# Eleven loads of weight sums on another DMA queue, and two products swapped, in an fp32-accurate streaming-encoder block on one Trainium2 core

## The chip, the cores and the metric

One core of a Trainium2 chip. The metric is the device time of one execution in microseconds; lower is better. The kernel is one program of 16129 instructions on TensorE (PE, with its weight loads listed as PEld), VectorE (DVE), ScalarE (ACT), GpSimd (POOL) and SyncE (SP). SP, ACT and POOL also issue DMAs, each through a queue of its own (SPq, ACTq; POOL's issues are listed as POOL).

## The reference

One layer over 512 tokens of width 1024, all in float32:

```
x = x + 0.5 * swiglu(rms_norm(x, ffn1_norm), gate1, up1, down1)
x = x + hybrid_mixer(rms_norm(x, mix_norm), ...)
x = x + 0.5 * swiglu(rms_norm(x, ffn2_norm), gate2, up2, down2)
return rms_norm(x, final_norm)
swiglu(h) = (silu(h @ w_gate) * (h @ w_up)) @ w_down
```

The hidden width of each feed-forward part (FFN) is 2816, that is 22 tiles of 128 or 11 pairs of tiles. The mixer (a projection, a state-space scan of 16 heads, chunked attention of 8 heads and an output projection) lies between the two FFNs, from about 300 to 700 us; the change doesn't touch it.

## The kernel before

**Split operands.** Each matrix product is made of three matmuls (`mm3`, L141 to L144, and L554 to L556): weight high part by activation high and low part, weight low part by activation high part. Each weight tile in SBUF is therefore split before use: ACT writes the high part (L272), DVE the rest (L274). `usplit` (L267) does so for the FFNs; its results rotate through four slots, so a split waits until PE is done with the tile four splits before.

**Seven products in place of eight.** In an FFN most of the work is a two-by-two block product done with seven products, P1 to P7 (Winograd's form of Strassen's scheme). Some need sums of weight blocks. They are made by DMAs that add into SBUF. For P5 of a pair of tiles d a buffer `view(d)` gets a first load (`first`, L329, a plain DMA) and one addition (`more`, L332, a DMA of POOL with `accum_op=add`). Once P5's split has read it, another addition makes P6's sum (L356), and once P6's split has read it, another makes P3's (L361). P7's sum is made the same way in a tile that P1 loaded (L358). P1, P2 and P4 use plain tiles (tag `raw`, four buffers, loaded through SP, L326). There are four such views; a new one takes the place of the one four before it, so its first load waits until the split of that one's P3 is done (`before`, L347 and L353).

**Order of the products.** `program` (L281) writes the order out by hand. With `plain` = 2 (FFN1) two pairs are done as plain products (A11 to A22) and pair 2 is the first by seven products; with `plain` = 1 (FFN2) pair 0 is plain. Then, pair by pair, come P5 and P1 of the next pair, P3 and P4 of this one, P6, P2, P7 of the next. After pairs 4 and 8 the products of a down block follow (the seven products again, on the down projection, steps "S", each with one or two half blocks written as (block, first pair)). FFN2 ends with a third down block whose second half has a view of its own for P6 (`LAST`, L349 to L354): a first load and two additions, with no split between them. In all 11 first loads are for down blocks, named `s<-ws` in the trace, and 19 for pairs (`s<-wgu`).

**Banks.** `run` (L545) gives a pair three PSUM banks: X for P1, P6, P7 and P4, L for P2, H for P5 and P3. ACT copies P1's (L560) and P6's (L563) result out of X, and the next product in X can't start before that. In the trace X is `mm`, L and H are `aux`.

**When things are issued.** `Stream.get` (L127) hands out the tiles in the order of the list, splits three ahead (`ws.look`), and issues a load or addition at most so many products ahead as its lead says (12 for a pair's first load, 14 for the last view's, 5 to 10 for others). The text of the program is, however, only a priority. A planner puts each instruction on its engine's queue when, by its own costs, its inputs and buffers are ready and the engine is free, the earlier in the text first. On the chip each queue then runs in that fixed order.

Of the kernel before, what the change touches and what calls it, by code (L numbers as in the profile page):

```python
# [37 lines left out]
def hybrid_block(ctx: ExitStack, tc, xT, xt, par, wgu1, wd1, ws1, win, wdt, wv, wo, rbt, wgu2, ws2, fin, out):  # L38
    nc = tc.nc
    V, S, G, T = nc.vector, nc.scalar, nc.gpsimd, nc.tensor  # L40
# [4 lines left out]
    def sb(tag, shape, dt=F32, bufs=1):  # L45
        uid[0] += 1
        return pool.tile(shape, dt, tag=tag, name=f"{tag}_{uid[0]}", bufs=bufs)
# [62 lines left out]
    class Stream:  # L110
# [16 lines left out]
        def get(self):  # L127
            i = self.used
            self.used += 1
            while self.done < min(len(self.jobs), i + 1 + self.look):  # L130
                job = self.jobs[self.done]
                job.move(0, True)
                job.parts = job.split()
                self.done += 1
            for n in range(self.done, min(len(self.jobs), i + 18)):
                self.jobs[n].move(n - i)
            return self.jobs[i].parts
# [95 lines left out]
    def wide_tile(g, dt=F32R):  # L233
        if g not in wide or wide[g][0] != dt:
            wide[g] = dt, sb(f"s{g}", [P, GROUPS[g], SEQ], dt)
        return wide[g][1]
# [30 lines left out]
    def usplit(src):  # L267

        i = turn[0] % 4
        turn[0] += 1  # L270
        hi = sb(f"xw{2 * i}", list(src.shape), F32R)
        S.copy(out=hi, in_=src)  # L272
        lo = sb(f"xw{2 * i + 1}", list(src.shape), F32R)
        V.tensor_tensor(out=lo, in0=src, in1=f(hi), op=ALU.subtract)  # L274
        return hi, lo
# [5 lines left out]
    def program(plain, by_tokens):  # L281


        if plain == 1:
            out = [("A11", 0), ("A21", 0), ("A12", 0), ("P1", 1), ("P5", 1), ("A22", 0), ("P6", 1), ("P2", 1), ("P7", 1)]
        else:
            out = [(a, d) for d in range(plain) for a in ("A11", "A21", "A12", "A22")]
            out += [(p, plain) for p in ("P5", "P1", "P6", "P2", "P7")]
        out = [("P", p, d) for p, d in out]
        ends = [b for _, b in BLOCKS[:2]]  # L290
        for d in range(plain + 1, ND):
            if d - 1 not in ends:
                out += [("P", p, e) for p, e in (("P5", d), ("P1", d), ("P3", d - 1), ("P4", d - 1))]
            out += [("P", p, d) for p in ("P6", "P2", "P7")]
            if d in ends:

                down = [("S", ends.index(d), p, (0, 1)) for p in DOWN]
                out += down[:1] + [("P", p, d) for p in ("P3", "P4")] + down[1:6]
                out += [("P", p, d + 1) for p in ("P5", "P1")] + down[6:]
        last = [("P", p, ND - 1) for p in ("P3", "P4")]  # L300
        if by_tokens == 3:
            return out + [("S", 2, "P5", (0,))] + last + [("S", 2, p, (0,)) for p in ("P1", "P2")] + [
                ("S", 2, p, (1,)) for p in ("P1", "P5")] + [("S", 2, "P6", (0, 1)), ("S", 2, "P2", (1,))] + [
                ("S", 2, p, (0, 1)) for p in ("P7", "P3", "P4")]
        out += [("D", 2, 0, 0)] + last + [("D", 2, 1, 0), ("D", 2, 0, 1), ("D", 2, 1, 1)]
        return out + [("D", 2, o, c) for o in range(2, KD) for c in range(2)]

    def ffn_weights(wgu, plain, by_tokens, wst, wd=None):


        bufs, jobs, views = {}, {}, []
        LAST = (2, ND - 1)

        def view(d):
            if d not in bufs:
                i = views.index(d)
                m = 2 if type(d) is int else min(2, BLOCKS[d[0]][1] - d[1])
                bufs[d] = wide_tile((40, 52)[i // 2 % 2], F32)[:, 2 * (i % 2):2 * (i % 2) + m]
                if type(d) is int:
                    bufs[d] = bufs[d].rearrange("p a (k c) -> p a k c", c=P)  # L320
            return bufs[d]

        def whole(key, src):
            def go():
                bufs[key] = sb("raw", list(src.shape), bufs=4)
                nc.sync.dma_start(out=bufs[key], in_=src)  # L326
            return go

        def first(d, src):  # L329
            return lambda: nc.sync.dma_start(out=view(d), in_=src)  # L330

        def more(get, src):  # L332
            return lambda: G.dma_start(out=get(), in_=src, accum_op=ALU.add)  # L333

        def product(p, d, A):

            sum_ = lambda: view(d)
            raw = {"P1": "g", "P2": "g2", "P4": "u2"}.get(p)
            if p[0] == "A":
                n = ("A11", "A12", "A21", "A22").index(p)  # L340
                j = Job(lambda: usplit(bufs[p, d]), (6, "raw", whole((p, d), A[n])))
            elif raw:
                j = Job(lambda: usplit(bufs[raw, d]), (6 if p == "P1" else 5, "raw",
                                                       whole((raw, d), A[("P1", "P2", "", "P4").index(p)])))
            elif p == "P5":
                views.append(d)
                before = jobs["P3", views[-5]] if len(views) > 4 else jobs.get(("A21", 0))  # L347
                j = Job(lambda: usplit(view(d)), (12, before, first(d, A[2])), (7, None, more(sum_, A[3])))
            elif p == "P6" and d == LAST:  # L349

                v = d + (2,)
                views.append(v)
                j = Job(lambda: usplit(view(v)), (14, jobs["P3", views[-5]], first(v, A[2])),  # L353
                        (10, None, more(lambda: view(v), A[3])), (6, None, more(lambda: view(v), A[0])))  # L354
            elif p == "P6":
                j = Job(lambda: usplit(view(d)), (6, jobs["P5", d], more(sum_, A[0])))  # L356
            elif p == "P7":
                j = Job(lambda: usplit(bufs["g", d]), (6, jobs["P1", d], more(lambda: bufs["g", d], A[2])))  # L358
            else:
                v = d + (2,) if d == LAST else d  # L360
                j = Job(lambda: usplit(view(v)), (6, jobs["P6", d], more(lambda: view(v), A[1])))  # L361
            jobs[p, d] = j
            if p == "P7":
                jobs["P1", d].holds = j
            ws.jobs.append(j)

        for step in program(plain, by_tokens):
            if step[0] == "P":
                p, d = step[1:]
                product(p, d, wgu[d])  # L370
            elif step[0] == "S":
                n, p, pieces = step[1:]
                for a in [BLOCKS[n][0] + 2 * c for c in pieces]:
                    product(p, (n, a), [wst[i, :, a:min(a + 2, BLOCKS[n][1]), :] for i in range(4)])
            else:
                n, o, c = step[1:]
                if c == 0:
                    a, b = 2 * BLOCKS[n][0], 2 * BLOCKS[n][1]
                    ws.add(wd[o, :, a:b, :], b - a, P)
                    late = ws.jobs.pop() if (n, o) in ((2, 0), (2, 1)) else None  # L380
                    if late:
                        jobs["late", o] = late
                elif ("late", o) in jobs and n == 2:
                    ws.jobs.append(jobs["late", o])
# [70 lines left out]
    def ffn(xc, n_plain, early, by_tokens, rc, between, after):  # L455
# [177 lines left out]
        pss = {}  # L633
        past = False
        for step in program(n_plain, by_tokens):
            if step[0] == "S":
                n, p, pieces = step[1:]
# [793 lines left out]
```

## Time and profile before

| | |
|---|---|
| median of 3 runs | 1032.14 us (1031.85 to 1036.27) |
| profiled execution | 1035.34 us |
| its span, first to last instruction | 1033.6 us |
| mean granted TensorE clock | 0.993 of full |
| PE busy | 1007.9 us, 98% of the span |
| DVE, ACT, POOL busy | 810.2, 587.8, 163.7 us |
| DMA through SP's and ACT's queues / POOL's | 96.74 + 4.86 MB / 60.04 MB |

The times are of executions of the whole program. The profiled execution is one more, 3.2 us above the median of the others; all durations of single instructions come from it. Times in the rows are microseconds from the start of its span, durations of groups nanoseconds. PE is busy nearly throughout, so the rows of interest are those in which it waits or runs at a lower clock.

### The profile page before, as it was taken

The numbers are of one execution on the slowest core, as the hardware profiler recorded it, in microseconds if no ns is written. First come the engines' busy times: TensorE is split into PE (matmuls) and PEld (weight loads), VectorE is DVE, ScalarE is ACT, GpSimd is POOL, SyncE is SP. The second block draws the span as 40 slices with busy tenths as digits, with TensorE's granted clock in tenths as the row PEclk, the third lists the DMA queues.
The fourth block names the chain that finished last, engine by engine and source line by source line (L and its number), as shares of the span: only waits on it lengthen the run. The fifth ranks groups of instructions, "written<-read, shape, count | busy, mean of one in ns | idle before, by whom it ended". The sixth has DMA issues, their size and how long they took to land. (4 is left out here: it accounts for less than half of the span.)

```text
span 1033.6 us, 16129 instructions
## 1 busy us (share of the span) xinstructions
PE 1007.9 (98%) x6154; PEld 888.6 (86%) x6154; DVE 810.2 (78%) x1353; ACT 587.8 (57%) x926; POOL 163.7 (16%) x186
## 2 busy tenths in 40 slices
PE   8999999999999999999999999999999999999895
PEld 7889989998898777778878778879999899988884
DVE  7868876887676698978867999797688668876587
ACT  7555535654474456646656876666655356544445
POOL 1111121111110013323201111101211111111110
PEclk9999999999999999999999999999999999999988
DMA  8969989998652321222232223755898889988842
GB/s 309 290 160 210 218 185 228 224 203 211 147 122 91 102 82 62 71 73 69 71 98 71 82 83 102 230 131 128 191 211 209 196 209 231 209 213 202 167 107 99
DMA packets 48221, 162.66 MB, mean 157 GB/s; under 512 B 5264, under 2 KB 6032, under 8 KB 48144
## 3 DMA queue, kind: packets, MB, share of 16 engines
q0 software_dynamic: 16848, 60.04, 33.2%
q1 hardware_dynamic: 28992, 96.74, 27.1%
q10 hardware_dynamic: 2304, 4.86, 1.5%
q8 instruction: 48, 0.79, 0.3%
q14 instruction: 29, 0.24, 0.1%
HBM read 159.52 MB, written 2.10 MB: 156 GB/s over the span
## 5 line engine op out<-in xcount | busy, mean ns | idle before, releaser
L555 PE MATMUL mm<-s,xw 128*128 128x256 f32 x1824 | 231.6, 284 | 6.4 <-ACT fu L563 4.6
L555 PEld LDWEIGHTS mm<-s,xw 128*128 128x128 f32 x1824 | 224.9, 192 | 7.6 <-ACT fu L563 5.0
L272 ACT CAST xw<-raw 128x1024 fp32r<-128x1024 f32 (+1 forms) x127 | 131.5, 1036 | 138.3 <-PE mm L555 56.0
L274 DVE TENSOR_TENSOR xw<-raw,xw 128x1024 fp32r<-128x1024 f32 (+1 forms) x127 | 152.7, 1204 | 69.4 <-ACT xw L272 69.4
L555 PE MATMUL aux<-s,xw 128*128 128x256 f32 x1368 | 174.5, 283 | 0.6 <-DVE xw L274 0.6
L555 PEld LDWEIGHTS aux<-s,xw 128*128 128x128 f32 x1368 | 169.0, 192 | 1.9 <-DVE xw L274 0.8
L142 PE MATMUL mm<-xw,whi 128*128 128x512 f32 x364 | 149.1, 410 | 0.0
L143 PE MATMUL mm<-xw,whi 128*128 128x512 f32 x364 | 144.3, 397 | 0.0
L274 DVE TENSOR_TENSOR xw<-s,xw 128x1024 fp32r<-128x1024 f32 (+1 forms) x87 | 104.6, 1202 | 50.5 <-ACT xw L272 50.4
L144 PE MATMUL mm<-xw,wlo 128*128 128x512 f32 x364 | 144.0, 396 | 0.0
L272 ACT CAST xw<-s 128x1024 fp32r<-128x1024 f32 (+1 forms) x87 | 90.0, 1035 | 92.1 <-DMA s<-wgu 27.7
L333 POOL DMA_DIRECT2D s<-wgu x57 | 52.1, 934 | 314.6 <-DMA s<-wgu 133.6
L84 ACT CAST whi<-raw 128x512 fp32r<-128x512 f32 (+1 forms) x104 | 62.1, 601 | 65.3 <-PE mm L143 47.2
L86 DVE TENSOR_TENSOR wlo<-raw,whi 128x512 fp32r<-128x512 f32 (+1 forms) x104 | 74.3, 716 | 13.8 <-ACT whi L84 13.2
L142 PEld LDWEIGHTS mm<-xw,whi 128*128 128x128 f32 x364 | 68.5, 188 | 16.2 <-issue 2.2
L144 PEld LDWEIGHTS mm<-xw,wlo 128*128 128x128 f32 x364 | 68.4, 188 | 16.1
L143 PEld LDWEIGHTS mm<-xw,whi 128*128 128x128 f32 x364 | 68.5, 188 | 15.8 <-issue 1.2
L333 POOL DMA_DIRECT2D s<-ws x31 | 27.1, 873 | 163.3 <-DVE xw L274 65.8
L144 PE MATMUL aux<-xw,s 128*128 128x512 f32 x106 | 41.8, 394 | 0.0
L143 PE MATMUL aux<-xw,s 128*128 128x512 f32 x106 | 41.7, 394 | 0.0
L142 PE MATMUL aux<-xw,s 128*128 128x512 f32 x106 | 41.7, 394 | 0.0
L903 POOL TENSOR_TENSOR fu<-dt,tri 128x512 fp32r<-128x512 f32 x16 | 18.9, 1190 | 95.6 <-PE aux L954 45.5
(294 smaller groups left out, 1743.9 us busy)
## 6 DMA issues: line engine op xcount, KB each, us to landing
raw<-wgu SPq DMA_DIRECT2D x68, 512.0 KB, 5.8
s<-wgu POOLq DMA_DIRECT2D x57, 512.0 KB, 6.5
raw<-win SPq DMA_DIRECT2D x28, 512.0 KB, 3.5
s<-ws POOLq DMA_DIRECT2D x27, 512.0 KB, 5.7
raw<-ws SPq DMA_DIRECT2D x27, 512.0 KB, 4.7
s<-wgu SPq DMA_DIRECT2D x19, 512.0 KB, 5.0
raw<-wgu POOLq DMA_DIRECT2D x19, 512.0 KB, 6.2
raw<-wo SPq DMA_DIRECT2D x12, 512.0 KB, 3.7
```

Of the source, the lines that this page charges most:

```text
L84: S.copy(out=hi, in_=src)
L86: V.tensor_tensor(out=lo, in0=src, in1=f(hi), op=ALU.subtract)
L142: T.matmul(ps, lhsT=sh, rhs=mh, start=start, stop=False, skip_group_check=skip)
L143: T.matmul(ps, lhsT=sh, rhs=ml, start=False, stop=False, skip_group_check=skip)
L144: T.matmul(ps, lhsT=sl, rhs=mh, start=False, stop=stop, skip_group_check=skip)
L272: S.copy(out=hi, in_=src)
L274: V.tensor_tensor(out=lo, in0=src, in1=f(hi), op=ALU.subtract)
L333: return lambda: G.dma_start(out=get(), in_=src, accum_op=ALU.add)
L555: T.matmul(ps[:, j * HS:(j + 1) * HS], lhsT=sw[:, j, k], rhs=m, start=(p in ("P1", "P2", "P5") and j == 0 and k == 0 and n == 0), stop=(k ...
L903: G.tensor_tensor(out=r, in0=f(src[:, c, h0:h0 + 4]).unsqueeze(2).broadcast_to([P, 4, P]), in1=tri.unsqueeze(1).broadcast_to([P, 4, P]), o ...
```

## The change

The first loads of down blocks go through POOL's queue in place of SP's: for a pair `d` is a number, for a down block a pair of numbers, and the test tells these apart. In FFN1's first pair by seven products (pair 2; the branch for `plain` = 1 is another) P2 comes before P6. Since the list of loads and splits and the order of the matmuls both come from `program`, both follow.

```diff
@@ in program
         else:
             out = [(a, d) for d in range(plain) for a in ("A11", "A21", "A12", "A22")]
-            out += [(p, plain) for p in ("P5", "P1", "P6", "P2", "P7")]
+            out += [(p, plain) for p in ("P5", "P1", "P2", "P6", "P7")]
         out = [("P", p, d) for p, d in out]
@@ in ffn_weights
         def first(d, src):
-            return lambda: nc.sync.dma_start(out=view(d), in_=src)
+
+            q = nc.sync if type(d) is int else G
+            return lambda: q.dma_start(out=view(d), in_=src)
```

## Rows read from the trace of the kernel before

**Rows 1.** The page, busy us of each engine (share of the span) and instructions
```profile
PE 1007.9 (98%) x6154; PEld 888.6 (86%) x6154; DVE 810.2 (78%) x1353; ACT 587.8 (57%) x926; POOL 163.7 (16%) x186
```

**Rows 2.** Stretches: busy us of PE, PEld, DVE, ACT, POOL; PEclk, DMA share, GB/s
```profile
60.00:80.00 20.00, 18.21 (x148) 17.82 (x149) 13.83 (x19) 11.24 (x15) 3.52 (x4) 1.00 0.73 175
...
980.00:985.00 5.00, 2.39 (x11) 2.39 (x12) 2.89 (x5) 3.00 (x4) 0.00 (x0) 0.56 0.30 58
985.00:990.00 5.00, 5.00 (x25) 4.57 (x25) 3.31 (x4) 2.06 (x3) 0.00 (x0) 0.76 0.17 52
```

**Rows 3.** PE near the end: start, length, instruction, [idle before <-releaser]
```profile
974.93 3.04 PE L555 MATMUL aux<-s,xw 128*128 128x256 f32 x24
982.61 5.24 PE L555 MATMUL mm<-s,xw 128*128 128x256 f32 x24 [4.64 <-ACT fu L563]
```

**Rows 4.** Timeline of ACT near the end
```profile
981.03 1.04 ACT L272 CAST xw<-s 128x1024 fp32r<-128x1024 f32 x1 [6.35 <-DMA s<-wgu]
981.98 0.58 ACT L563 COPY fu<-mm 128x512 f32<-128x512 f32 x1
```

**Rows 5.** Timeline near the end: SP's queue, then DVE, then POOL
```profile
960.49 0.33 SPq L330 DMA_DIRECT2D s<-ws  x1
...
964.67 1.22 DVE L274 TENSOR_TENSOR xw<-s,xw 128x1024 fp32r<-128x1024 f32 x1 [1.06 <-ACT xw L272]
...
966.91 0.88 POOL L333 DMA_DIRECT2D s<-ws  x1 [8.43 <-DMA s<-ws]
...
971.52 0.88 POOL L333 DMA_DIRECT2D s<-ws  x1 [3.73 <-DMA s<-ws]
972.14 1.14 POOL L333 DMA_DIRECT2D s<-wgu  x1
```

**Rows 6.** Timeline of FFN1's pair 2: PE, then ACT
```profile
59.97 1.58 PE L555 MATMUL aux<-s,xw 128*128 128x256 f32 x11 [0.63 <-DVE xw L274]
63.34 3.13 PE L555 MATMUL mm<-s,xw 128*128 128x256 f32 x24 [1.79 <-ACT fa L560]
...
53.75 1.05 ACT L272 CAST xw<-s 128x1024 fp32r<-128x1024 f32 x1 [7.15 <-DMA s<-wgu]
...
57.28 1.03 ACT L272 CAST xw<-raw 128x1024 fp32r<-128x1024 f32 x1
...
62.71 0.58 ACT L560 COPY fa<-mm 128x512 f32<-128x512 f32 x1
```

**Rows 7.** Issues of L330 and L333 (ns min/median/max); DMA queues; DMA issues
```profile
L330 SPq DMA_DIRECT2D s<-ws x11: 327/328/328, 29.7 to 960.5; - x11
...
L333 POOL DMA_DIRECT2D s<-ws x31: 865/867/891, 42.9 to 1003.9; - x31
...
q0 software_dynamic: 16848, 60.04, 33.2%
q1 hardware_dynamic: 28992, 96.74, 27.1%
...
outT<-s SPq DMA_DIRECT2D x8, 256.0 KB, 2.8
...
s<-ws POOLq DMA_DIRECT2D x4, 256.0 KB, 6.2
...
s<-ws SPq DMA_DIRECT2D x2, 256.0 KB, 4.6
```

**Rows 8.** Start of the program: PE, POOL, SP's queue, ACT, a stretch
```profile
8.23 0.50 PE L142 MATMUL mm<-s,xw 128*128 128x512 f32 x1 [0.39 <-ACT s L149]
...
19.96 1.02 POOL L333 DMA_DIRECT2D s<-wgu  x1 [18.45 <-DMA s<-wgu]
...
29.75 0.33 SPq L330 DMA_DIRECT2D s<-ws  x1
...
34.67 0.21 ACT L1123 ACTIVATE dt<-par 128x16 f32<-128x16 f32 x1
...
8.00:10.00 2.00, 1.49 (x5) 1.04 (x6) 1.79 (x3) 2.00 (x5) 0.00 (x0) 1.00 1.01 408
```

## The prediction

> **What bounds the kernel now.** I read the page's busy times first: TensorE (PE) works 1007.9 of 1033.6 us [rows 1], so nothing that another engine saves can pay except inside PE's 25.7 us of idle time, plus what a lower clock costs. Next come the waits of PE in order of time. Two places matter to this change.
>
> The large one is near the end. PE finishes the product P2 of pair 10 at 977.97 (974.93 + 3.04) and starts P7 at 982.61: 4.64 us idle, released by ScalarE's copy at L563 [rows 3]. That copy empties the PSUM bank into which P7 must write, and it is itself only 0.58 us long; it stands behind the split of P3's weight sum, which waited 6.35 us for a DMA [rows 4]. While PE stood idle the granted clock went to the lower of its two levels (1.2 instead of 2.4 GHz): the means are 0.56 and 0.76 of full in the next two stretches [rows 2], and P7's 24 matmuls took 5.24 us where P2's took 3.04 [rows 3], 2.20 us more. The place costs 4.64 + 2.20 = 6.84 us.
>
> Why is P3's sum late? Its last addition needs only that VectorE has done with P6's split, at 965.89 (964.67 + 1.22). But POOL issues it at 972.14, behind two additions for the last block's P6 sum, and each of those waits for the transfer before it: for the first load, which SP issued at 960.49, until 966.91, then for the next until 971.52 [rows 5]. POOL's queue is in order, so P3's addition stood 6.25 us behind waits that aren't its own.
>
> The small place is the first Strassen pair, FFN1's pair 2: 0.63 us before part of P2 and 1.79 us before P6, the latter for ScalarE's copy of P1 (L560), which runs at 62.71 because ScalarE first made P2's split at 57.28 and others. ScalarE had stood 7.15 us for P6's sum until 53.75 [rows 6]. The clock was 1.00 in the stretch that holds the longer of the two [rows 2].
>
> **Part one, the order of products.** P2 needs a plain weight tile, P6 a sum that lands at 53.75. With P2 first its split can be done inside ScalarE's 7.15 us of waiting, so it no longer stands at 57.28 ahead of the copy: 1.05 us less in that backlog. And P2's 24 matmuls (some 2.9 us) stand between P1 and P6, which share a bank, so the copy of P1 is covered. That removes 0.63 + 1.79 = 2.42 us. In return P6 and P7, which share that bank too, become neighbours: a copy of 0.58 us [rows 4] is exposed unless PE has other work there. Net -1.8 us. Bounds: -2.4 (all covered by the next pair's P5) to +0.6 (nothing saved, the copy added). No load is added: the same tiles move, two in another order, and the later use of P6's sum only loosens it.
>
> **Part two, the queue of 11 loads.** SP loses 11 issues of 0.33 us, POOL gains 11 of 0.87 us [rows 7], 9.5 us on an engine that is busy 163.7 of 1033.6 us [rows 1]. Nine of the eleven fall where PE doesn't wait (the other two follow below); there I price them at nothing, the cover being the products split ahead. If that cover went, each would cost its 0.54 us.
>
> The last one is in the chain above. It can start no earlier than at 960.49, when its buffer comes free. Through POOL the chain starts 0.54 us later by issue; by landing, SP's 256 KB loads took 4.6 us and POOL's 256 KB additions 6.2 [rows 7], so 0.5 to 2.1 us. I take 0.5, since a plain load is nearer to a plain load.
>
> What decides is the order in which the planner then puts POOL's instructions. It queues what is ready first by its own clock. It put both additions of the block ahead of P3's, so by that clock load and addition fitted between the buffer's release and P6's split, 965.89 - 960.49 = 5.4 us; on the chip they took 11.03 [rows 5]. The quickest kind of 256 KB transfer in these rows takes 2.8 us in the median [rows 7]; two of those would be 5.6. An estimate as quick as that leaves next to no margin, and the first transfer now also costs POOL's 0.54 us. So I hold it a little likelier than not that P3's addition moves ahead of at least the second of the two. Then it is issued right behind the first, at 966.91 + 0.88 + 0.5 = 968.3 instead of 972.14. Keeping its 8.89 us to landing, the copy at L563 ends 3.8 us earlier, at 978.7; PE waits 0.8 instead of 4.64 us, less than the 1.79 that left the clock alone. Gain 3.8 + 2.2 = 6.0 us. Bounds: 6.8 (ahead of both) and, with the order kept, a loss of 0.5 to 2.1.
>
> At the other end, the very first of the eleven has no buffer to wait for. SP issued it at 29.75, before PE had begun the first pair, and ScalarE ran an instruction of L1123, of the mixing stage, at 34.67: the planner hoists what is ready into any free queue. POOL is free from 1.5 us to 19.96 [rows 8]. So I expect this load at about 2 us, with its addition behind it, among the loads that PE waits for: PE waits for x at 8.23, and the DMA engines are full (1.01) [rows 8]. By the queues' shares a plain MB takes 0.271 x 1033.6 / 96.74 = 2.90 us of all 16 engines and an added MB 0.332 x 1033.6 / 60.04 = 5.72 [rows 7]; 0.524 MB each, so 1.5 and 3.0 us. Bounds 0 and 4.5 us; I take the load whole and a third of the addition, +2.5 us, as the addition meets loads that are partly ahead of PE.
>
> The Trainium skill speaks against the move: "DMA: Bandwidth & Descriptors", section "Issuing engines are not separate DMA queues", says that DMAs of SP, ScalarE and GpSimd share the same engines and that another issuer saves only issue time. The issue rows agree and even show a dearer issue on POOL; what the rule would make of the sum is the fourth rival below.
>
> **The sum.** -6.0 - 1.8 + 2.5 = -5.3 us. The profiled execution took 1035.34 us (span 1033.6) and would take 1030.0; the median shown, 1032.14, is 3.2 below it, and the same difference gives 1026.8.
>
> **Rivals.**
> *The order on POOL is kept.* P3's addition stays last; the wait at L563 remains and grows by 0.5. -1.8 + 2.5 + 0.5 = +1.2: 1033.3. For it: POOL's issue adds little. Against: the thin margin. Chance 0.23.
> *The start decides (slower).* Load and addition both go ahead of what PE needs first, 4.5 us, and PE stands long enough for the clock to fall as it did at the end, 2.2 more; with the order kept the total is 4.5 + 2.2 + 0.5 - 1.8 = +5.4: 1037.5. It decides once the addition is issued before the second weight tile has landed. For it: POOL idle and full DMA engines; against: the x loads are issued first. Chance 0.12.
> *The swap does nothing.* PE's order is the planner's, and the trace already shows part of P2 ahead of P6 [rows 6]. Then 2.5 - 6.0 = -3.5: 1028.6. Chance 0.10.
> *The queue does nothing.* No order changes and no load is hoisted; only the swap is left, -1.8: 1030.3. By the rule on shared engines it would be this one. Chance 0.08.
>
> **How the numbers follow.** My forecast, with P3's addition moved ahead, has 0.47. Its own range is 1023.5 (no hoist, or both additions passed) to 1029 (the start at its full 4.5). About 0.5%, 5.2 us, is what a measurement of this kernel tells from no change; the forecast lies just past it, so 0.37 of its 0.47 counts as faster and 0.10 as within. With 0.03 from the two last rivals with no price at the start, faster is 0.40; within 0.48; slower 0.12. The range 1022.0 to 1035.5 takes in all but the slower rival and the ends.
>
> **What would show it.** Right: P3's `s<-wgu` addition on POOL directly behind the last block's first `s<-ws` addition or ahead of it; no wait near 4.6 us at L563; full clock there; an `s<-ws` load on POOL before 3 us and PE's first products 1 to 3 us later; P2 whole between P1 and P6 of pair 2. Wrong: the three POOL rows in their old order with the wait at 981, or a new wait at a block's start, where P6's sum was already the last to come.

## The result, and the profile after

The changed kernel takes 1029.07 us (median of 10 runs, 1028.27 to 1030.25), the kernel before 1033.65 (10 runs, 1031.75 to 1036.27). The ratio is 0.9949, 95% interval 0.9938 to 0.9960: about 5.3 us less by the ratio, 4.6 by the medians. The profiled execution of after took 1028.88 us, span 1026.8, against 1035.34 and 1033.6: 6.8 us of span to account for. Lines of the code stand two further down in after (L555 is L557, L563 is L565; a first load is at L332, an addition at L335).

The page of after, the busy times first:

```profile
PE 1007.0 (98%) x6154; PEld 888.7 (87%) x6154; DVE 810.8 (79%) x1353; ACT 588.1 (57%) x926; POOL 168.9 (16%) x197
```

TensorE (PE) does the work of [rows 1] in a shorter span; what went is idle time and time at the lower clock. POOL has 11 more instructions, the first loads.

**The end.** POOL's timeline in after (start, length, instruction, idle time before it and its releaser):

```profile
960.93 0.56 POOL L332 DMA_DIRECT2D s<-ws  x1 [2.34 <-DVE xw L274]
965.61 0.85 POOL L335 DMA_DIRECT2D s<-ws  x1 [4.12 <-DMA s<-ws]
966.40 0.96 POOL L335 DMA_DIRECT2D s<-wgu  x1
970.20 0.86 POOL L335 DMA_DIRECT2D s<-ws  x1 [2.84 <-DMA s<-ws]
```

In [rows 5] the two `s<-ws` additions came first, each behind a landing, and P3's `s<-wgu` third, at 972.14. Now P3's goes between them, at 966.40. The split of P6 that precedes all this began at 963.59 before and at 963.69 after, so the absolute times can be compared. Timelines of ScalarE (ACT), then of PE, in after:

```profile
975.16 1.05 ACT L272 CAST xw<-s 128x1024 fp32r<-128x1024 f32 x1 [0.38 <-PE mm L557]
976.11 0.58 ACT L565 COPY fu<-mm 128x512 f32<-128x512 f32 x1
...
975.03 3.04 PE L557 MATMUL aux<-s,xw 128*128 128x256 f32 x24
977.91 3.04 PE L557 MATMUL mm<-s,xw 128*128 128x256 f32 x24
```

P3's split no longer waits for a DMA, the copy ends before P2 does, and P7 follows P2 with no gap, in 3.04 instead of 5.24 us [rows 3, 4]. The clock in that stretch was 0.56 [rows 2]; the same stretch of after, columns as there:

```profile
980.00:985.00 5.00, 5.00 (x31) 4.36 (x31) 3.47 (x6) 3.12 (x4) 0.87 (x1) 1.00 0.26 63
```

From the split of P6 to the split of the last block's P1 it is 24.22 us before and 17.23 after: 6.99 us. These splits are, before and then after:

```profile
963.59 1.05 ACT L272 CAST xw<-s 128x1024 fp32r<-128x1024 f32 x1 [1.34 <-PE aux L555]
987.81 1.05 ACT L272 CAST xw<-raw 128x1024 fp32r<-128x1024 f32 x1 [3.78 <-issue]
...
963.69 1.05 ACT L272 CAST xw<-s 128x1024 fp32r<-128x1024 f32 x1 [1.35 <-issue]
980.92 1.05 ACT L272 CAST xw<-raw 128x1024 fp32r<-128x1024 f32 x1 [1.82 <-PE mm L557]
```

**The front.** PE in FFN1's pair 2, in after:

```profile
59.32 3.04 PE L557 MATMUL mm<-s,xw 128*128 128x256 f32 x24
62.20 3.04 PE L557 MATMUL aux<-s,xw 128*128 128x256 f32 x24
65.08 3.04 PE L557 MATMUL mm<-s,xw 128*128 128x256 f32 x24
67.96 1.72 PE L557 MATMUL aux<-s,xw 128*128 128x256 f32 x13
69.67 3.13 PE L557 MATMUL mm<-s,xw 128*128 128x256 f32 x24
72.64 1.48 PE L557 MATMUL aux<-s,xw 128*128 128x256 f32 x11
```

These are P1, P2 whole, P6, a part of the next pair's P5, P7, the rest of P5; the gaps of 0.63 and 1.79 us [rows 6] are gone, and the part of P5 hides the copy between P6 and P7.

**The start.** The timelines of POOL, ACT and PE there, in after; the last row is PE's first product before:

```profile
1.41 0.70 POOL L332 DMA_DIRECT2D s<-ws  x1 [0.26 <-issue]
8.21 0.62 ACT L703 CAST xw<-raw 128x512 fp32r<-128x512 f32 x1 [2.60 <-DMA raw<-wgu]
8.24 0.88 POOL L335 DMA_DIRECT2D s<-ws  x1 [5.72 <-DMA s<-ws]
8.88 0.79 PE L142 MATMUL mm<-s,xw 128*128 128x512 f32 x1 [3.19 <-ACT xw L703]
9.90 0.63 PE L142 MATMUL mm<-s,xw 128*128 128x512 f32 x1
...
6.18 0.50 PE L142 MATMUL mm<-s,xw 128*128 128x512 f32 x1 [1.06 <-ACT xw L701]
```

The first of the first loads moved from 29.75 [rows 8] to 1.41, its addition to 8.24, and both stand among the first weights. PE's first product begins at 8.88, 2.70 us later than before (6.18). In after the first ten products take 4.43 us, most of them 0.63 each, where later ones take 0.40 each from 13.6 us on; before, the first ten took 3.64, with two short waits for x among them. That is the lower clock. The trace of after has no record of the clock ahead of 13.4 us (a row for that stretch shows 1.00 for want of one), but in the run with the queue alone, described below, the first products look the same after a wait of 3.33 us, and the record shows 0.50 (columns as in [rows 2]):

```profile
9.00:11.00 2.00, 2.00 (x5) 1.61 (x6) 1.92 (x3) 2.00 (x4) 0.23 (x1) 0.50 1.07 427
```

To compare kernels I cut the span of each one's profiled execution at four splits of ScalarE (in pair 1 the one of A22, in pair 3 the one of P2, the end's two as above). All times in us; the ratio is of measured times, to the kernel before run beside it, with its 95% interval.

| kernel | start: to A22 of pair 1 | front: to P2 of pair 3 | middle: to P6 of FFN2's last pair | end: to P1 of the last block | span | ratio |
|---|---|---|---|---|---|---|
| before | 30.59 | 46.04 | 886.96 | 24.22 | 1033.6 | 1 |
| after | 33.83 | 43.09 | 886.77 | 17.23 | 1026.8 | 0.9949 (0.9938 to 0.9960) |
| swap alone | 30.84 | 43.10 | 887.48 | 24.64 | 1031.8 | 0.9972 (0.9960 to 0.9983) |
| queue alone | 33.36 | 43.42 | 889.08 | 17.83 | 1029.9 | 0.9953 (0.9935 to 0.9970) |
| after, start's load on SP | 30.08 | 43.08 | 887.61 | 17.23 | 1023.8 | 0.9922 (0.9907 to 0.9937) |
| end's load alone on POOL | 30.91 | 44.98 | 887.13 | 17.22 | 1026.1 | 0.9941 (0.9924 to 0.9959) |
| two in order, others tied | 30.37 | 43.37 | 884.67 | 22.21 | 1026.4 | 0.9947 (0.9931 to 0.9963) |
| after, P3 last, others tied | 33.19 | 43.11 | 884.40 | 25.07 | 1031.7 | 1.0009 (0.9992 to 1.0026) |
| start's load alone on POOL | 33.73 | 43.39 | 887.51 | 21.97 | 1032.4 | 1.0011 (0.9995 to 1.0027) |
| after, addition held, others tied | 33.97 | 43.11 | 884.42 | 17.23 | 1024.6 | 0.9936 (0.9914 to 0.9957) |
| two in order, no other tie | 31.33 | 47.29 | 887.58 | 17.22 | 1028.2 | 0.9948 (0.9929 to 0.9966) |
| start's load on SP, text order | 30.20 | 43.09 | 884.41 | 17.22 | 1020.8 | 0.9895 (0.9877 to 0.9913) |
| swap, all on SP, text order | 31.02 | 43.07 | 884.79 | 17.23 | 1021.8 | 0.9892 (0.9872 to 0.9912) |
| text order alone | 30.42 | 43.37 | 884.08 | 17.22 | 1020.8 | 0.9880 (0.9857 to 0.9903) |

After against before: +3.24 at the start, -2.95 at the front, -0.19 in the middle, -6.99 at the end, +0.17 behind it; sum -6.72, the difference of the spans.

The columns differ in how far they repeat. The end without a wait is 17.22 or 17.23 in eight kernels. The start is 30.08 to 31.33 in the nine kernels that leave its load on SP and 33.19 to 33.97 in the five that hoist it; the means are 3.0 apart. Two entries contain a spell at the lower clock that the kernels beside them don't have: the middle of the queue alone (granted clock 0.50 from 671.2 to 674.5 us) and the front of two in order, no other tie (0.50 from 65.7 to 69.0).

### The profile page after: what moved, and what is told of

The parts are those of the page before. It is cut to its first block, busy times and chain, and to the rows that moved or that the text cites. A ratio compares the mean times of both kernels' runs of the same rounds, so it can differ in the third digit from the quotient of the medians.

```text
span 1026.8 us, 16130 instructions
## 1 busy us (share of the span) xinstructions
PE 1007.0 (98%) x6154; PEld 888.7 (87%) x6154; DVE 810.8 (79%) x1353; ACT 588.1 (57%) x926; POOL 168.9 (16%) x197
## 4 chain that ended last, share of the span: by engine, by line
PE 85%; DVE 10%; ACT 2%; DMA 2%; issue 1%; SPq 0%; ACTq 0%; DVEq 0%
PE mm L557 21%; PE aux L557 16%; PE mm L142 11%; PE mm L144 11%; PE mm L143 11%; PE aux L144 3%; PE aux L143 3%; PE aux L142 3%; DVE fs L850 2%; DMA raw<-wgu 2%; DVE wlo L86 1%; DVE xw L274 1%; PE aux L1210 1%; PE aux L974 1%; PE aux L765 1%
## 5 line engine op out<-in xcount | busy, mean ns | idle before, releaser
L557 PE MATMUL mm<-s,xw 128*128 128x256 f32 x1824 | 229.3, 283 | 0.0
L557 PEld LDWEIGHTS mm<-s,xw 128*128 128x128 f32 x1824 | 222.9, 191 | 0.8 <-ACT fu L565 0.2
L557 PE MATMUL aux<-s,xw 128*128 128x256 f32 x1368 | 174.3, 283 | 0.0
L557 PEld LDWEIGHTS aux<-s,xw 128*128 128x128 f32 x1368 | 168.9, 192 | 1.2 <-DVE s L569 0.2
L335 POOL DMA_DIRECT2D s<-wgu x57 | 51.2, 920 | 307.0 <-DMA s<-wgu 118.7
L335 POOL DMA_DIRECT2D s<-ws x31 | 26.9, 867 | 136.7 <-DMA s<-ws 51.3
```

The lines of the kernel that those rows point to most:

```text
L557: T.matmul(ps[:, j * HS:(j + 1) * HS], lhsT=sw[:, j, k], rhs=m, start=(p in ("P1", "P2", "P5") and j == 0 and k == 0 and n == 0), stop=(k ...
```

## The experiments

**The swap alone.** The change's first hunk, nothing else:

```diff
-            out += [(p, plain) for p in ("P5", "P1", "P6", "P2", "P7")]
+            out += [(p, plain) for p in ("P5", "P1", "P2", "P6", "P7")]
```

> Only the order of FFN1's first products by seven: P2 before P6; every first load stays on SP. Theory (three separate terms: the start pays 3.2 us for the hoisted load, the front gives back 2.9, the end gives 7.0): this kernel has the front term alone. In its trace P2 of pair 2 runs whole between P1 and P6 with no gaps of 0.63 and 1.79 us, the start is as before (PE's first product at 6.2 us), and the wait of 4.6 us at L563 stands. Time 2 to 3 us below the kernel before. Rival (the gain of the whole change comes with the swap, for instance because the planner's later slots move with it): 4 us or more below. Rival (the swap gives nothing, since the split of P6 is late whatever stands before it): within 0.6 us.

Measured: 1031.90 us against 1034.98, ratio 0.9972. The front is 43.10, 2.94 shorter than before; the wait at the end stands (5.20 us). The first theory's figure holds; both rivals fall.

**The queue alone.** The change's second hunk, with the old order of products:

```diff
+            q = nc.sync if type(d) is int else G
+            return lambda: q.dma_start(out=view(d), in_=src)
```

> Only the queue: the ten first loads on POOL, the old order of the first products. Theory: start +3.2, end -7.0, and at pair 2 the gaps of 0.63 and 1.79 us shrink or vanish by themselves, since SP no longer carries the load and all of PE's work comes 3.2 us later; so 3.8 us below the kernel before if the gaps stay, up to 6.5 if they go. Against the changed kernel it is then 0 to 2.9 us slower. Rival (the swap is needed for the end too): the wait of 4.6 us at the last view's block stands and the time is 2 to 4 us above the kernel before.

Measured: 1029.66 us, ratio 0.9953. The end is 17.83 us (0.60 us of idle time left in it), so the swap isn't needed there. The surprise is the front: 43.42, although P2 stands behind P6 again. PE there in this kernel:

```profile
58.90 3.04 PE L557 MATMUL mm<-s,xw 128*128 128x256 f32 x24
61.78 1.72 PE L557 MATMUL aux<-s,xw 128*128 128x256 f32 x13
63.49 3.13 PE L557 MATMUL mm<-s,xw 128*128 128x256 f32 x24
```

No gap. So the front's gain has two sufficient causes, and inside the change the swap is worth only 43.42 - 43.09 = 0.33 us. The trace of before shows what the queue does there. POOL, the kernel before:

```profile
41.54 0.86 POOL L333 DMA_DIRECT2D s<-wgu  x1 [17.76 <-DMA s<-wgu]
42.91 0.89 POOL L333 DMA_DIRECT2D s<-ws  x1 [0.51 <-DMA s<-ws]
44.37 0.88 POOL L333 DMA_DIRECT2D s<-wgu  x1 [0.57 <-DVE fa L500]
```

The third row is P6's addition, for which ScalarE waited until 53.75 [rows 6]; it took 9.27 us to land. The second row belongs to the load that the change hoists to the start. In the run with the queue alone it is no longer there: P6's addition is issued 2.8 us later, at 47.16, and lands after 5.38 us, at 52.54, 1.1 us earlier than before, while PE is 2.8 us later.

**The whole change without the hoisted load.**

```diff
-            q = nc.sync if type(d) is int else G
+            q = nc.sync if type(d) is int or (by_tokens, d) == (2, (0, 0)) else G
```

> The whole change, but FFN1's first s<-ws load stays on SP; the other nine go through POOL. Theory (the hoisted load and the addition behind it take the weights' share of the DMA engines in the first 17 us and cost 3.2 us): PE's first product is back at 6.2 us, the front and end gains stay (-2.9 and -7.0), and the time is 3 us below the changed kernel (about 1026) and 7 to 10 below the kernel before. If the milder start is given back at pair 2, because the splits there are then the late party again, it is only 0 to 1 us below the changed kernel. Rival (the later start comes from POOL's queue as such, or differs from run to run): no difference to the changed kernel at the start.

Measured: 1026.39 us, ratio 0.9922. The start is back at 30.08 with PE's first product at 6.19, and front and end keep their gains. The price of the start is thus that one load's, with the addition behind it, and it isn't given back at pair 2, as the swap holds that place.

**One load moved, the last.**

```diff
-            return lambda: nc.sync.dma_start(out=view(d), in_=src)
+            q = G if d == LAST + (2,) else nc.sync
+            return lambda: q.dma_start(out=view(d), in_=src)
```

> The kernel before with one load moved: the first s<-ws load of the last block's view alone goes through POOL. Theory (the end's gain is the order on POOL: P3's s<-wgu addition is issued ahead of the last view's second addition): the order tips in the same way with this one load, the wait of 4.6 us at L563 is gone with the half-clock stretch behind it, and the time is 6 to 7 us below the kernel before, with the start and the gaps of pair 2 as before. Rival (the end gains because SP's queue is relieved of all the first loads, or because the additions find the DMA engines emptier over the whole run): one load gives a fraction, 0 to 1.5 us.

Measured: 1028.52 us, ratio 0.9941; the end is 17.22, and the order on POOL is that of after. (Of the two gaps of pair 2 the 0.63 is gone and 1.58 us of the other is left, though nothing was changed there.) One load of the eleven carries the whole gain of the end, so relief of SP over the run isn't its cause.

**Order or queue?** Three kernels were to set the order by hand. Their edit, by a slip, did more than their expectations say: an addition for which none was given to stand behind was tied behind the last one without a name, so that almost all additions on POOL came in the order of the program text.

```diff
-        def more(get, src):
-            return lambda: G.dma_start(out=get(), in_=src, accum_op=ALU.add)
+        seen = {}
+        def more(get, src, name=None, behind=None):
+            def go():
+                if behind in seen:
+                    with tc.issue_after(seen[behind]):
+                        r = G.dma_start(out=get(), in_=src, accum_op=ALU.add)
...
+                seen[name] = r.ins
```

First, before with the last view's second addition behind P3's (`more(lambda: view(v), A[0], None, "P3")`):

> The kernel before with every first load on SP and the old order of products; only the last view's second addition is put behind P3's addition on POOL. Theory (the end's gain is the order of two additions on POOL, whichever queue carries the first loads): the wait of 4.6 us at L563 and the half-clock stretch go, the stretch from P6's split to P1's split of the last block falls from 24.2 us to 17.2, and the time is 6 to 7 us below the kernel before, as with the one load moved. Rival (the earlier landing of the first load on POOL's queue is what makes room): the stretch stays above 22 us and the time is within 2 us of the kernel before.

Measured: 1028.42 us, ratio 0.9947, but the end is 22.21, as the rival said; the gain lies in the front and the middle. The extra ties had put another `s<-ws` addition ahead, and P3's was issued 6.30 us after P6's split, against 8.55 before and 2.71 in after. Taken alone, this run spoke against me.

Second, after with P3's addition behind both of the last view's, and these given the lead of their first load:

> The whole change, but P3's addition is put behind both additions of the last view, as it stood before; the first loads stay on POOL. Theory: the wait comes back, since P3's addition waits for the first two landings again; the stretch from P6's split to P1's split is 22 to 25 us instead of 17.2, and the time is 4 to 7.5 us above the changed kernel. Rival (the queue gives the gain): it stays within 1 us of the changed kernel.

Measured: 1034.86 us, ratio 1.0009, against 0.9949 for the changed kernel: 0.6% more, some 6 us. POOL, then PE (this view ends inside P7), in this kernel:

```profile
964.98 0.85 POOL L340 DMA_DIRECT2D s<-ws  x1 [6.49 <-DMA s<-ws]
969.93 0.85 POOL L340 DMA_DIRECT2D s<-ws  x1 [4.10 <-DMA s<-ws]
970.53 1.15 POOL L340 DMA_DIRECT2D s<-wgu  x1
...
980.97 2.29 PE L566 MATMUL mm<-s,xw 128*128 128x256 f32 x9 [5.89 <-ACT fu L574]
```

With P3's addition third again the wait is back, 5.89 us, though all eleven first loads go through POOL (the expectations say ten; the traces have eleven). First loads on POOL give nothing at the end unless the order changes with them.

Then the first of these again, without the slip: `if behind and behind in seen`, so that only one addition is tied.

> The kernel before; first loads on SP, old order of products; the last view's second addition behind P3's addition on POOL, and no other edge (the run that was meant to do this had, by a slip of its edit, tied every other addition to the one before it in the order of the program text too). Theory (PE waits at the end by as much as P3's addition lands later than about 12.7 us after the split of P6, whatever sets that): P3's addition now has one landing less ahead of it, about 4.2 us, so it lands at +12 to +14 instead of +17.3, the wait is 0 to 1.3 us instead of 4.6, and the time 4 to 7 us below the kernel before. Rival (the first load must go through POOL for that): it lands at +15 or later, the wait stays above 2.3, and the time is less than 3.5 below.

Measured: 1029.21 us, ratio 0.9948, end 17.22. POOL, ACT and PE in this kernel:

```profile
967.85 0.88 POOL L340 DMA_DIRECT2D s<-ws  x1 [7.76 <-DVE xw L274]
968.76 0.88 POOL L340 DMA_DIRECT2D s<-wgu  x1
972.63 0.86 POOL L338 DMA_DIRECT2D s<-ws  x1 [3.00 <-DMA s<-ws]
...
977.33 1.05 ACT L272 CAST xw<-s 128x1024 fp32r<-128x1024 f32 x1 [1.05 <-DMA s<-wgu]
...
976.54 3.04 PE L564 MATMUL aux<-s,xw 128*128 128x256 f32 x24
979.42 3.04 PE L564 MATMUL mm<-s,xw 128*128 128x256 f32 x24
```

The wait is gone and P7 takes 3.04 us, with every first load on SP and the old order of products. Here the split of P3 still waits 1.05 us for the addition, and PE doesn't feel it: this is the edge. The theory holds, and the confounded run fits too once all are put side by side by when P3's addition lands (both columns of times from the start of P6's split):

| kernel | addition issued | landed | PE idle | landed less idle |
|---|---|---|---|---|
| after, P3 last, others tied | 9.83 | 18.59 | 5.89 | 12.70 |
| swap alone | 8.27 | 17.90 | 5.20 | 12.70 |
| before | 8.55 | 17.34 | 4.64 | 12.70 |
| two in order, others tied | 6.30 | 16.13 | 3.43 | 12.70 |
| start's load alone on POOL | 7.26 | 15.70 | 3.00 | 12.70 |
| queue alone | 3.87 | 13.06 | 0.60 | 12.46 |
| two in order, no other tie | 3.56 | 12.04 | 0 | |
| after, start's load on SP | 3.16 | 11.99 | 0 | |
| after | 2.71 | 10.89 | 0 | |
| text order alone | 2.71 | 7.92 | 0 | |

PE waits by as much as that landing passes 12.7 us; before it, an earlier landing is worth nothing. (The four kernels not in the table land at 8.0 to 12.0 and have no wait.) What the end loses beyond the idle time is the lower clock: 24.22 - 17.23 - 4.64 = 2.35 us in the kernel before. The granted clock there is 0.50 from 980.6 to 987.4, and PE is busy 4.79 us of that stretch; at the full clock that work takes half as long, an estimate of 2.4 us. In the four others with one long wait the loss is 1.55 to 2.2, by the same reckoning 1.4 to 2.2. In the run with 0.60 us in two parts the clock stays at 1.00, and there is no loss.

**The start's load alone.**

```diff
-            return lambda: nc.sync.dma_start(out=view(d), in_=src)
+            q = G if (by_tokens, d) == (2, (0, 0)) else nc.sync
+            return lambda: q.dma_start(out=view(d), in_=src)
```

> The kernel before with FFN1's first s<-ws load alone on POOL, old order of products. Theory (the load is hoisted to the start and takes its addition with it: 3 us there; but that addition then no longer stands between the two additions of P6 of pair 2, so that the front's wait goes without the swap, as in the run with the queue alone, where that stretch shortened by 2.6 us): start later by 2.8 to 3.2 us, front shorter by 2.6, end as before: 0 to 1 us above the kernel before. Rival (the front's gain is the swap's alone): 2.5 to 3.5 us above.

Measured: 1035.10 us against 1033.45, ratio 1.0011 (0.9995 to 1.0027): from 0.5 us below to 2.8 above. By the profile the start is 3.14 longer and the front, without the swap, 2.65 shorter, as the theory says; the time alone doesn't exclude 2.5, the low edge of the rival. Moving this load buys nothing by itself: what it costs at the start it gives back 50 us later.

**The load, or the addition behind it?** The changed kernel, with that addition named and held behind the next pair's first (`more(sum_, A[3], (by_tokens, d), (2, 2) if (by_tokens, d) == (2, (0, 0)) else None)`); the slip above ties the other additions here as well.

> The whole change, but the addition behind FFN1's first s<-ws load is held behind the next pair's first s<-wgu addition on POOL, so that at the start the load stands alone. My forecast charged 1.5 us to the load and 1.0 to the addition. If the load (512 KB that land by 8 us, in the time in which the first weights land) is what makes the start late, PE's first product stays at 8.9 us and the time within 0.7 us of the changed kernel; if the addition (landing at 16.9 us) has a share of a third, the first product stays at 8.9 but the split of A22 comes 0.8 to 1.2 us earlier and so does the end; if the addition were all, the start is 2.5 us or more earlier.

POOL, then PE, at the start of this kernel:

```profile
1.40 0.70 POOL L332 DMA_DIRECT2D s<-ws  x1 [0.26 <-issue]
...
21.04 0.88 POOL L342 DMA_DIRECT2D s<-wgu  x1 [18.54 <-DMA s<-wgu]
21.63 1.19 POOL L340 DMA_DIRECT2D s<-ws  x1
...
8.31 0.79 PE L142 MATMUL mm<-s,xw 128*128 128x512 f32 x1 [3.29 <-ACT xw L712]
```

The addition is at 21.63 instead of 8.24, and A22's split still comes at 33.97 (33.83 in after). PE's first product comes 0.57 us earlier, at 8.31, but the lower clock lasts until 14.4 instead of 13.4 us, and the first 24 products take 8.42 us instead of 7.70. The kernel with P3 last had, by the slip, this addition held back too: its first product is at 8.89, its lower clock ends at 12.1, and its A22 comes at 33.19. The three kernels with load and addition at the start have 33.36 to 33.83, between the two. So the load alone makes the start late; a price of the addition doesn't show, and one of some tenths would be lost in what the clock does. The time, 1026.96 us, ratio 0.9936, is nonetheless lower than the changed kernel's: the middle is 884.42 us instead of 886.77. All three tied kernels have that (884.40 to 884.67), and no other had (886.77 to 889.08). So the slip had found something, and the next three runs follow it.

**The order of the text.** Every addition on POOL is tied behind the one traced before it:

```diff
-            return lambda: G.dma_start(out=get(), in_=src, accum_op=ALU.add)
+            def go():
+                if last_more:
+                    with tc.issue_after(last_more[-1]):
...
+                last_more.append(r.ins)
```

With the change's queue, but the start's load on SP:

> The changed kernel with FFN1's first s<-ws load on SP, and every addition on POOL tied behind the one before it in the order of the program text. Theory: start and front as with the load on SP (-3 against the changed kernel), the end at 17.2 us with P3's addition landing below +12, and the middle 2.0 to 2.5 us shorter than in the changed kernel, as in the three runs that had such a tie (the stretch from P2's split of FFN1's second pair to P6's split of the last pair was 884.4 to 884.7 there, 886.8 in the changed kernel): 1023 to 1025. Rival (the three runs' shorter middle had another cause, or a fixed order loses what a free one won): 1026 or more.

With the swap, and all first loads on SP:

> The kernel before with the swap of P2 and P6 and with every addition on POOL tied behind the one before it in the order of the program text; all first loads stay on SP, so the change's move of queue is left out. Theory (order on POOL is the whole gain, the queue of the first loads only a way to tip it): P3's addition lands below +12.7, the end at 17.2, and the time within 1 us of the same kernel with its first loads on POOL, that is 1023 to 1026. Rival (POOL's queue for the first loads has a worth of its own, by SP's issues or by earlier landings): 2 us or more above that kernel.

With neither:

> The kernel before with every addition on POOL tied behind the one before it in the order of the program text, and nothing else: first loads on SP, old order of products. Theory (the front's wait, like the end's, is an addition that stands on POOL behind one that nobody waits for yet; the swap is only another way past it): the gaps of 0.63 and 1.79 us at pair 2 go without the swap, and the time is within 1 us of the kernel with the swap and the text's order (1023.2), some 10 below the kernel before. Rival (the front needs the swap): 2 to 3 us above that kernel, 1025.5 to 1026.

Measured: 1023.45 us (ratio 0.9895), 1023.15 (0.9892) and 1022.91 (0.9880), the last on another chip than the first two. All three meet the theory: neither the queue nor the swap adds anything that these runs can tell once the additions stand in the order in which their sums are used. The third, a few lines against the kernel before, is as fast as the two others and 1.2% below before, where the change won 0.5%. POOL in its trace, at the front and at the end, then PE at the end:

```profile
44.16 0.87 POOL L338 DMA_DIRECT2D s<-wgu  x1 [22.62 <-DVE xw L274]
48.04 0.86 POOL L338 DMA_DIRECT2D raw<-wgu  x1 [3.01 <-DVE xw L274]
...
960.58 0.86 POOL L338 DMA_DIRECT2D s<-wgu  x1 [6.92 <-DVE xw L274]
962.62 1.78 POOL L338 DMA_DIRECT2D s<-ws  x2 [1.18 <-DMA s<-ws]
...
969.21 3.04 PE L564 MATMUL aux<-s,xw 128*128 128x256 f32 x24
972.09 3.04 PE L564 MATMUL mm<-s,xw 128*128 128x256 f32 x24
```

P6's addition of pair 2 is now the first of its group, at 44.16, and its split follows at 49.64 instead of 53.75 [rows 6]; P3's addition goes ahead of both `s<-ws`, which still make their own date. Of the middle's 2.9 us (886.96 - 884.08), 2.1 stand in the waits between 600 and 710 us: PE is idle 2.38 us of that stretch in before, 2.20 in after and 0.31 here. All of PE's waits there, around the end of the mixer, are for VectorE (in before 0.85 us for x, L1288, at 680.55 and 0.62 for s, L198, at 701.64), none directly for an addition. Why the order of additions removes them wasn't tried, and stays open.

## Why the prediction was right, and where not

The direction, the place of the large gain and the range held. The three terms were each undersized by 0.7 to 1.2 us, in different directions, so that the sum of spans came out at -6.7 against -5.3. That the ratio nonetheless gives -5.3 is luck: the profiled execution of before stood 1.7 us above the median of its ten runs, that of after 0.2 below.

- **The end, -6.0, measured -6.99.** The step "the planner moves P3's addition ahead of the second of the two" was held a little likelier than not, and is what happened. Two sizes in it were off. The chain was to start 0.5 us later through POOL; the first load landed at 964.97, 1.3 us earlier than in before, having taken 4.05 us. (That the queue made it quicker isn't shown: in the kernels without ties it took 4.0 to 5.4 us through POOL and 4.3 to 5.8 through SP.) And 0.8 us of waiting was to remain; P3's addition was issued at 966.40, not 968.3, and landed 1.8 us ahead of the edge. That the order does it, and the queue is only a way to tip it, was argued then; the two kernels with the order set either way show it.
- **The front, -1.8, measured -2.95.** The step that charged the copy between P6 and P7 (0.58 us) failed: PE had part of P5 to put there. The lower bound of -2.4 was passed: the two gaps account for 2.42 of the 2.95, and where the rest lies wasn't found. And the cause was only half seen: the swap does it alone (-2.94), but so does moving the hoisted load's addition out of the way of P6's on POOL (-2.62), and in the changed kernel the swap adds 0.33. The cuts repeat well enough for that: the kernels without gaps have 43.07 to 43.11 with the swap and 43.37 to 43.42 without it.
- **The start, +2.5, measured +3.24.** The hoist was foreseen: issue "at about 2 us" (1.41), first products 1 to 3 us later (2.70). The step "the load whole and a third of the addition" had the parts wrong: holding the addition back gained nothing that shows, so the load alone costs about 3 us. Its share of the queues' time, 1.5 us, was the wrong price. It is issued beside the first weights and lands with them (7.93 and 8.19); these arrived at 5.08 before, so PE pays the delay of the tile for which it waits, 3.1 us, not a fair share of the traffic. And the term had no price for the clock, which only a rival had: PE stood 3.19 us, and its first ten products ran at the lower level. At the later pace of 0.23 us from one to the next they would take 2.3 us instead of 4.43; against before the loss is smaller (3.64 there), since before had waits for x in that stretch.
- **The other nine loads, nothing.** The middle moved by 0.19 us. The cost of their issue was set too high: a first load took POOL 0.56 us in the median, not the 0.87 of an addition.
- **The base.** Sum and ratio agree (-5.3 both); the time, 1029.07 against 1026.8 forecast, is off mostly by the base: the three runs shown had a median of 1032.14, ten have 1033.65.

Of the rivals, the kept order is what the kernel with P3 last shows (1.0009); it came out near the price given for it (1033.3, or +0.1% on the median shown), but only with the help of the other ties, which shorten that kernel's middle by 2.4 us. The swap alone and the queue alone each did something, against the third and the fourth. On the fourth the Trainium skill ("DMA: Bandwidth & Descriptors", section "Issuing engines are not separate DMA queues") says that another issuer saves only the time of the issue, and with the order fixed these runs agree: first loads through POOL and through SP give 1023.45 and 1023.15 us. What it leaves open is that another issuer changes the order of an in-order engine, and here that was 7 us. The start as the decider, at 4.5 us and a lower clock, came to 3.24 with the lower clock; it didn't decide.

## What to carry to other kernels

Where accumulating transfers of several sums share one issuing engine, look at the order of that queue before its length: set it to the order in which the sums are used, as a planner that goes by readiness may put a sum that nobody needs yet ahead of the one for which TensorE will wait. Before you price a load that a planner may hoist, look at what is landing at that moment: beside the first weights, 512 KB cost about 3 us here; issued at 29.13 us, in the run with the start's load on SP, the same load cost nothing that shows. And cut the span at a few fixed instructions: one number for the whole would have shown neither that the change paid 3.2 us nor that its swap was worth 0.3.

## What the runs showed that I had not expected

- The wait at the end is a straight line: PE idle = landing of P3's addition - 12.70 us in five kernels, from 3.00 to 5.89 us.
- An addition of 512 KB on POOL took 5.2 us to land where it was issued ahead of the others (960.58 to 965.78, text order alone), and 8.2 us where another's landing overlapped with it (966.40 to 974.58, after).
- PE's first products took 0.63 us each in after, following a wait of 3.19 us, and 0.40 in the run with the start's load on SP, following 0.49. All five kernels that hoist the load ran their first products at the lower clock. The late start costs 0.5 us more than the later first product (3.24 against 2.70).
- Kernels with the wait at the end also vary more, though with so unequal numbers of runs that isn't shown: the kernel before ranged from 1029.81 to 1038.02 us over 23 runs, and its wait's length differs between kernels that leave that place alone (4.64, 5.20, 3.00 us); text order alone ranged from 1022.05 to 1023.28 over 5.
